# State-space scan of a bidirectional encoder block on one Trainium2 core: chunks laid out by place in their block of 8, and a scan instruction for the states between blocks

## The chip, the cores and the metric

The kernel runs on one core of one Trainium2 chip. The metric is the device time of one launch in microseconds. Three runs of the kernel before took 2667.21 to 2672.29 us, median 2671.31 us.

## The reference

One encoder layer runs on two sequences of width 1024: a prompt of 2048 positions and a sample of 512, with the same weights. Half of the mixer's channels go through a two-dimensional Fourier transform, the other half through a bidirectional state-space scan, which is what the change touches. A channel group of 16 drives 64 complex states; each state is multiplied by a constant complex number per position and gets an input added.

```python
def s5_direction(u_c, a_re, a_im, log_dt, b_re, b_im, c_re, c_im, reverse):
    lam = lax.complex(jnp.minimum(a_re, A_RE_MAX), a_im)
    dt = jnp.exp(log_dt)[:, None]
    a_bar = jnp.exp(lam * dt)
    b_bar = ((a_bar - 1.0) / lam)[..., None] * lax.complex(b_re, b_im)
    bu = jnp.einsum("blgh,gph->blgp", u_c, b_bar)
    a_seq = jnp.broadcast_to(a_bar, bu.shape)
    _, h = lax.associative_scan(_scan_combine, (a_seq, bu), axis=1, reverse=reverse)
    return jnp.einsum("blgp,ghp->blgh", h, lax.complex(c_re, c_im)).real
...
    h = rmsnorm(x, g_mix_norm) * (1.0 + scale1) + shift1
    z = h @ w_in
    y_f = fourier_mixer(z[..., :D_FOURIER], w_fourier, b_fourier)
    y_s = s5_mixer(z[..., D_FOURIER:], ...)      # y_fwd + y_bwd + D u, gelu, GLU
    merged = jnp.concatenate([rmsnorm(y_f, g_fourier_out), rmsnorm(y_s, g_ssm_out)], axis=-1)
    x = x + gate1 * (merged @ w_out)
    h = rmsnorm(x, g_mlp_norm) * (1.0 + scale2) + shift2
    ff = jnp.square(jax.nn.relu(h @ w_mlp_in + b_mlp_in)) @ w_mlp_out + b_mlp_out
    return x + gate2 * ff
```

## The kernel before

The work stands in four parts that follow one another. `mix_in` (stretch 0 to 328 us of the trace) norms the input, multiplies by `w_in`, folds the positions for the Fourier half and builds the tables of the scan: `ssm_params` (L145), `ssm_pre` (L206), and, as jobs between the folds, `scan_tables` (L123) and eight calls of `ssm_out` (L278). Then comes the scan itself together with the Fourier half (328 to 690 us), then `mix_out` (to 1117 us), then the MLP (to the end).

The scan works on columns of 8 positions. 2560 positions are 320 columns, 256 of the prompt and 64 of the sample; a matmul turns the 8 inputs of a column into its contribution to the state. The 32 channel groups go in 8 rounds `q` of `NQ = 4`. A round has a tile `V` of 128 partitions (64 states forward, 64 backward) x 2 (real, imaginary) x 4 groups x 321 columns, and these steps:

- `lead` loads the round's matrices and inputs, puts the columns in order on ScalarE (`un`), multiplies (`psV`), and copies to `V`, the backward half reversed.
- `step1` sweeps up over blocks of 8 columns, on VectorE: distances 1, 2 and 4, so that each block's last column holds the block's sum. Distance 1 is 16 instructions (L367), each multiplying by a scalar per partition and adding; distances 2 and 4 go through `axpy` (L374), which makes one complex multiply and add of four instructions (L378 to L381).
- `step2` carries the states between the 40 blocks, in two levels of 5 x 8: seven dependent `axpy` on 40 elements, then five steps on the five groups of eight (L388 to L405).
- `step3` sweeps down (distances 4, 2, 1), and three matmuls per group (`psY`) with the copies `S` of `V` give the output, which is copied (`y`) and stored.

The loop in `run` interleaves the rounds: round q's `lead`, round q-1's `step2`, round q-2's `step3`, round q's `step1`, and between them `slot`, which issues one unit of the Fourier half and of its part of the output projection (`beside`) and one column block of the conditioning matrix (`pa`). All of it is laid on the engines' queues by a scheduler (L1511) that reorders instructions when the kernel is built; every engine then runs its own queue strictly in order. The scan's pools `ssa` and `ssm` lie where the pools of `mix_in` lay (`rs.close()`, L874), so its tiles wait for the last reader of those, `ssm_out` among them. Tables go through DRAM: `ssm_out` writes `sO` on ScalarE's queue, `lead` reads it on SP's.

## Time and profile before

| | us |
|---|---|
| median of three runs | 2671.31 |
| the profiled execution's own time | 2667.14 |
| its span, first to last instruction | 2665.3 |
| TensorE (PE) busy | 2528.9 (95%) |
| VectorE (DVE) busy | 1714.6 (64%) |
| ScalarE (ACT) busy | 1277.0 (48%) |
| GpSimd (POOL) busy | 588.4 (22%) |

The profile comes from one execution. Busy time is the union of an engine's instructions; a busy TensorE may still run at the lower of its two clocks, which the granted clock tells. L numbers are lines of the kernel before; a helper's line stands for all its callers, so tiles' names tell the place.

### The profile page before, as it was taken

Reading aid. Unit: us, or ns where it says so; the run is one execution under the profiler, and the core shown is the slowest. Engines: PE = TensorE matmul, PEld = TensorE weight load, DVE = VectorE, ACT = ScalarE, POOL = GpSimd, SP = SyncE. Lnnn points to the kernel's source line nnn. Section 1 sums busy time; section 2 is a strip of 40 time slices with the busy share of each in tenths; the row PEclk is TensorE's granted clock in tenths of the full one; section 3 lists DMA queues with packets and bytes.
Section 4 is the critical chain, followed back from the end, with each engine's and each line's share of the span. In section 5 each row is a group of like instructions: output and inputs, shape, how many; then the busy total and the mean of one; then the engine's idle time right before and its main releaser. Section 6 shows DMA issues by size and latency. Waiting matters only on the chain.

```text
span 2665.3 us, 35595 instructions
## 1 busy us (share of the span) xinstructions
PE 2528.9 (95%) x12643; PEld 2285.8 (86%) x12643; DVE 1714.6 (64%) x2935; ACT 1277.0 (48%) x2227; POOL 588.4 (22%) x464
## 2 busy tenths in 40 slices
PE   6879999997999999899999999999999999999997
PEld 2767877766777878799999999999999999999997
DVE  7789599999548877446767973354346533644454
ACT  2633344544444434635544546355445573654443
POOL 3322110024355443733700001004000020130000
PEclk8979988878999999999999999999999999999999
DMA  7634476466777898777666777686667776766664
GB/s 272 209 125 144 133 233 195 151 217 237 262 264 248 296 317 291 276 245 272 226 221 221 263 256 263 222 277 231 225 223 282 242 245 227 274 229 222 229 229 163
DMA packets 276739, 623.40 MB, mean 234 GB/s; under 512 B 66256, under 2 KB 108304, under 8 KB 274768
## 3 DMA queue, kind: packets, MB, share of 16 engines
q1 hardware_dynamic: 237264, 547.16, 60.8%
q10 hardware_dynamic: 32944, 59.36, 5.9%
q0 software_dynamic: 6352, 14.60, 1.7%
q8 instruction: 100, 1.64, 0.2%
q14 instruction: 79, 0.65, 0.1%
HBM read 467.13 MB, written 153.89 MB: 233 GB/s over the span
## 4 chain that ended last, share of the span: by engine, by line
PE 49%; DVE 2%; issue 0%; ACT 0%; POOL 0%; DVEq 0%; ACTq 0%
PE acc L204 9%; PE acc L203 9%; PE acc L202 9%; PE pf L203 7%; PE pf L204 7%; PE pf L202 7%; DVE x L1439 0%; DVE big L1439 0%; PE pb L713 0%; PE pn L695 0%; DVE wl L1373 0%; DVE big L1291 0%; DVE big L1308 0%; DVE th L1324 0%; DVE ss L1277 0%
## 5 line engine op out<-in xcount | busy, mean ns | idle before, releaser
L1371 ACT CAST wh<-wr 128x512 fp32r<-128x512 f32 x672 | 414.8, 620 | 687.1 <-PE acc L203 346.7
L204 PE MATMUL pf<-th,wl 128*128 128x426 f32 (+1 forms) x1344 | 478.5, 357 | 9.1 <-POOL wl L1373 6.2
L203 PE MATMUL pf<-th,wh 128*128 128x426 f32 (+1 forms) x1344 | 481.1, 358 | 1.3 <-DVE th L1324 1.3
L202 PE MATMUL pf<-th,wh 128*128 128x426 f32 (+1 forms) x1344 | 481.0, 358 | 0.7 <-ACT x L1292 0.6
L203 PE MATMUL acc<-th,wh 128*128 128x426 f32 (+1 forms) x1344 | 478.3, 357 | 0.4 <-DVE th L1324 0.3
L202 PE MATMUL acc<-th,wh 128*128 128x426 f32 (+1 forms) x1344 | 474.5, 357 | 0.0
L204 PE MATMUL acc<-th,wl 128*128 128x426 f32 (+1 forms) x1344 | 466.9, 357 | 2.1 <-DVE wl L1373 2.0
L1391 DVE TENSOR_TENSOR big<-big,pf 128x426 f32<-128x426 f32 (+1 forms) x320 | 184.8, 596 | 250.0 <-PE pf L204 203.1
L1324 DVE TENSOR_TENSOR th<-big,th 128x1704 fp32r<-128x1704 f32 (+1 forms) x82 | 159.6, 1946 | 201.5 <-ACT th L1323 201.3
L204 PEld LDWEIGHTS pf<-th,wl 128*128 128x128 f32 x1344 | 253.8, 189 | 19.8 <-POOL wl L1373 6.9
L202 PEld LDWEIGHTS pf<-th,wh 128*128 128x128 f32 x1344 | 253.4, 189 | 11.1 <-issue 1.0
L204 PEld LDWEIGHTS acc<-th,wl 128*128 128x128 f32 x1344 | 253.2, 189 | 11.2 <-DVE wl L1373 2.8
L203 PEld LDWEIGHTS pf<-th,wh 128*128 128x128 f32 x1344 | 254.0, 189 | 10.0 <-DVE th L1324 1.5
L203 PEld LDWEIGHTS acc<-th,wh 128*128 128x128 f32 x1344 | 252.5, 188 | 9.5 <-DVE th L1324 1.1
L202 PEld LDWEIGHTS acc<-th,wh 128*128 128x128 f32 x1344 | 252.9, 188 | 9.0
L1230 POOL TENSOR_TENSOR q<-q,q 128x512 f32<-128x512 f32 x116 | 188.9, 1628 | 261.0 <-DMA q<-in_w 125.1
L709 POOL TENSOR_TENSOR r<-r,mh 128x4 f32<-128x4 f32 (+3 forms) x32 | 37.4, 1174 | 893.5 <-DVE r L708 883.9
L1398 POOL TENSOR_TENSOR big<-big 128x426 f32<-128x426 f32 (+1 forms) x128 | 144.4, 1133 | 398.2 <-ACT big L1397 397.6
L1373 DVE TENSOR_TENSOR wl<-wr,wh 128x512 fp32r<-128x512 f32 x168 | 123.3, 747 | 58.4 <-ACT wh L1371 51.5
L1323 ACT CAST th<-big 128x1704 fp32r<-128x1704 f32 (+1 forms) x82 | 132.5, 1616 | 0.7 <-PE acc L204 0.7
L1373 POOL TENSOR_TENSOR wl<-wr,wh 128x512 fp32r<-128x512 f32 x56 | 84.0, 1502 | 122.1 <-ACT wh L1371 105.9
L1324 DVE TENSOR_TENSOR th<-x,th 128x1704 fp32r<-128x1704 f32 (+1 forms) x23 | 44.6, 1938 | 83.6 <-ACT th L1323 83.6
(437 smaller groups left out, 4591.2 us busy)
## 6 DMA issues: line engine op xcount, KB each, us to landing
wl<-wL SPq DMA_DIRECT2D x224, 512.0 KB, 3.7
wr<-wS SPq DMA_DIRECT2D x192, 512.0 KB, 4.4
wr<-in_w SPq DMA_DIRECT2D x144, 512.0 KB, 4.5
wL<-wl SPq DMA_DIRECT2D x112, 512.0 KB, 2.9
q<-in_w SPq DMA_DIRECT2D x116, 256.0 KB, 4.4
wS<-q ACTq DMA_DIRECT2D x116, 256.0 KB, 3.9
wa<-in_w_ada SPq DMA_DIRECT2D x48, 512.0 KB, 5.5
big<-x1D SPq DMA_DIRECT2D x8, 1704.0 KB, 7.7
```

The source lines that it names most:

```text
L202: nc.tensor.matmul(out, l[0], r[0], start=start, stop=False)
L203: nc.tensor.matmul(out, l[0], r[1], start=False, stop=False)
L204: nc.tensor.matmul(out, l[1], r[0], start=False, stop=stop)
L709: nc.gpsimd.tensor_tensor(r[:m, js], r[:m, js], self.mh[:m, js], op=ALU.pow)
L1230: e.tensor_tensor(o, x, y, op=op)
L1323: nc.scalar.copy(th[0], src)
L1324: return th, v.tensor_tensor(th[1], src, th[0].bitcast(F32), op=ALU.subtract)
L1371: nc.scalar.copy(hi, r)
L1373: (nc.gpsimd if i % 2 and st["ph"] == 1 else v).tensor_tensor(lo, r, hi.bitcast(F32), op=ALU.subtract)
L1391: v.tensor_tensor(f[q], f[q], ps, op=op)
L1398: nc.gpsimd.tensor_tensor(f[q], f[q], f[q], op=ALU.mult)
```

## The change

Column b*8+j of a block b, place j, now lies at [j][b]: `V` is 128 x 2 x 4 x 9 x 40; a sweep at any distance takes whole runs of 40 neighbouring elements in place of every 2nd, 4th or 8th element. The order is made where `z` is stored, in the copies to `un`, and is undone in the copy to `y`; `V`, `S` keep it. The sweeps have the same number of instructions and elements as before; distance 2 is split by place and not by group.

Between blocks, `step2` turns each block's sum back by the phase that a block's constant has gained up to block b (a table of cosines and sines), runs a real first-order recurrence over the 40 blocks with one `tensor_tensor_scan` for the real and one for the imaginary part, and turns the result forward again. The multiplier of the recurrence, the constant's magnitude over 64 positions, is set to zero at blocks 0 and 32, where a sequence starts.

The table (cosine, sine, multiplier) is new: `ssm_params` computes magnitude and phase over 64 positions, `scan_tables` builds powers of the phase and, for each round, the table `RT`, which goes to DRAM (`s3`); `rload` brings a round's table back into the one tile `R` on SP's queue. The second level of powers (`BJ`) goes.

```diff
-def scan_tables(nc, tc, pk, tp, A8):
+def scan_tables(nc, tc, pk, tp, P, sR):
...
+    T4 = tp.tile([128, 4, 8, G], F32, tag="O", name="J")
+    J, K = ({k: T4[:, 2 * i + j] for j, k in enumerate("ri")} for i in range(2))
     with tc.tile_pool(name="sct", bufs=1) as tq:
-        powers(nc, tq, AJ, 0, 8)
         for k in "ri":
-            v.tensor_copy(BJ[k][:, 0], AJ[k][:, 7])
-        powers(nc, tq, BJ, 0, 8)
...
+            v.tensor_copy(J[k][:, 0], P["A8"][k][:, 0])
+        for j in (1, 2):
+            a = {x: J[x][:, j - 1] for x in "ri"}
+            cmul(nc, v, tq, J["r"][:, j], J["i"][:, j], a["r"], a["i"], a["r"], a["i"], [128, G], "pw1")
...
+        v.tensor_copy(r, J["r"][:, 0:3].rearrange("p j g -> p g j"))
+        v.tensor_scalar(i2[:, 0], J["i"][:, 0:3].rearrange("p j g -> p g j"), -1.0, None, op0=ALU.mult)
+        v.tensor_copy(i2[:, 1], J["i"][:, 0:3].rearrange("p j g -> p g j"))
+
...
+        for k in "ri":
+            v.tensor_copy(J[k][:, 1], P["U"][k])
+        powers(nc, tq, J, 1, 7)
+        cmul(nc, v, tq, K["r"][:, 1], K["i"][:, 1], J["r"][:, 7], J["i"][:, 7], J["r"][:, 1], J["i"][:, 1], [128, G], "pw1")
+        powers(nc, tq, K, 1, 4)
+    n = NQ
+    for q in range(G // n):
+        gs = slice(n * q, n * q + n)
+        T = tp.tile([128, 3, n, 40], F32, tag="o2", name="RT")
+        t = tp.tile([128, n, 40], F32, name="rt")
+        sh = [128, n, 5, 8]
+        w = lambda x: x.rearrange("p g (a j) -> p g a j", j=8)
+        ja = {k: bc(J[k][:, :, gs].rearrange("p j g -> p g j").unsqueeze(2), sh) for k in "ri"}
+        ka = {k: bc(K[k][:, 0:5, gs].rearrange("p a g -> p g a").unsqueeze(3), sh) for k in "ri"}
+        for c, (x, y, op) in enumerate((("r", "i", ALU.subtract), ("i", "r", ALU.add))):
+            v.tensor_tensor(w(T[:, c]), ja["r"], ka[x], op=ALU.mult)
+            v.tensor_tensor(w(t), ja["i"], ka[y], op=ALU.mult)
+            v.tensor_tensor(T[:, c], T[:, c], t, op=op)
+        nc.scalar.copy(T[:, 2], bc(P["R64"][:, gs].unsqueeze(2), [128, n, 40]))
+        nc.gpsimd.memset(T[:, 2, :, 0:33:32], 0.0)
+        nc.scalar.dma_start(sR[q], T)
+    return {"Ar": r, "Ai": i2}
...
+    R64, U = po.tile(sh, F32, name="R64"), {k: po.tile(sh, F32, name="U"+k) for k in "ri"}
+    v.tensor_scalar(x, x, 64.0, None, op0=ALU.mult)
+    v.tensor_scalar(th, th, 64.0, None, op0=ALU.mult)
+    exp_dve(nc, tp, R64, x, sh)
+    sincos_dve(nc, tp, U["r"], U["i"], th, sh)
...
+        un = ta.tile([128, NQ, 8, 40], F32, name="un", bufs=3)
+        nat = un[:, :, :, 0:32].rearrange("p g j (t h) -> p g t j h", h=2)
+        src = u[:, :, 0:256].rearrange("p g (t j s h) -> p g t j s h", t=4, j=8, s=4)
+        for sec, t in enumerate((slice(0, 4), slice(7, 3, -1), slice(8, 12), slice(15, 11, -1))):
+            for h in range(2):
+                nc.scalar.copy(nat[:, :, t, :, h], src[:, :, :, :, sec, h])
+        nc.scalar.copy(un[:, :, :, 32:40], u[:, :, 256:320].rearrange("p g (j c) -> p g j c", j=8))
+        un = un.rearrange("p g j b -> p g (j b)")
+
+        V = ta.tile([128, 2, NQ, 9, 40], F32, tag="V", name="V", bufs=3)
         for c in range(2):
             for j in range(NQ):
                 ps = net.ps([128, 320], "psV")
                 nc.tensor.matmul(ps, It[:, c, j], un[:, j], start=True, stop=True)
-                o = V[:, c, j, 1:321]
-                nc.scalar.copy(o[0:64], ps[0:64])
-                nc.scalar.copy(o[64:128, 0:256], ps[64:128, 255::-1])
-                nc.scalar.copy(o[64:128, 256:320], ps[64:128, 319:255:-1])
+                o = V[:, c, j, 1:9]
+                x = ps.rearrange("p (j b) -> p j b", j=8)
+                nc.scalar.copy(o[0:64], x[0:64])
+                nc.scalar.copy(o[64:128, :, 0:32], x[64:128, ::-1, 31::-1])
+                nc.scalar.copy(o[64:128, :, 32:40], x[64:128, ::-1, 39:31:-1])
+        if q == 0:
+            self.rload(0)
...
+            t4 = t.rearrange("p g (j b) -> p g j b", j=8)
+            nc.scalar.copy(t4[0:64], V[0:64, c, :, 0:8])
+            nc.scalar.copy(t4[64:128, :, :, 0:32], V[64:128, c, :, 7::-1, 31::-1])
+            nc.scalar.copy(t4[64:128, :, :, 32:40], V[64:128, c, :, 7::-1, 39:31:-1])
...
-            nc.scalar.copy(y[:, j], py)
+            nc.scalar.copy(y[:, j].rearrange("p (b j) -> p j b", j=8), py.rearrange("p (j b) -> p j b", j=8))
...
-            dst, x = V[:, :, :, o::2 * d], V[:, :, :, i::2 * d]
-            n = NQ if d == 4 else NQ // 2
-            sh = [128, 2, n, 160 // d]
-            for g in range(0, NQ, n):
-                G, r = slice(gs.start + g, gs.start + g + n), slice(g, g + n)
-                self.axpy(e, dst[:, :, r], x[:, :, r], x[:, ::-1, r], bc(P["Ar"][:, G, d - 1:d].unsqueeze(1), sh), bc(P["Ai"][:, :, G, d - 1:d], sh), sh, tag="t")
+            sh = [128, 2, NQ, 40]
+            for r in range(4 // d):
+                x = V[:, :, :, i + 2 * d * r]
+                dst = V[:, :, :, o + 2 * d * r]
+                self.axpy(e, dst, x, x[:, ::-1], bc(P["Ar"][:, gs, k:k + 1].unsqueeze(1), sh), bc(P["Ai"][:, :, gs, k:k + 1], sh), sh, tag="t")
...
-            self.sweep(b, d, b["V"][:, :, :, 1:321], True)
+            self.sweep(b, d, b["V"][:, :, :, 1:9], True)
...
-        P, tp, gs, e, n = self.P, self.tp, b["gs"], self.nc.vector, NQ
-        W = tp.tile([128, 2, n, 40], F32, tag="W", name="W")
-        W5 = W.rearrange("p c g (a b) -> p c g a b", b=8)
-        e.tensor_copy(W, b["V"][:, :, :, 8:321:8])
-        sh = [128, 2, n, 5]
-        br = bc(P["Br"][:, gs, 0:1].unsqueeze(1), sh)
-        bi = bc(P["Bi"][:, :, gs, 0:1], sh)
-        for j in range(1, 8):
-            x = W5[:, :, :, :, j - 1]
-            self.axpy(e, W5[:, :, :, :, j], x, x[:, ::-1], br, bi, sh)
...
+
+        V, R, e = b["V"], self.R, self.nc.vector
+        sh = [128, 2, NQ, 40]
+        cos, sin = (bc(R[:, i].unsqueeze(1), sh) for i in range(2))
+        T = V[:, :, :, 8]
+        W = self.tp.tile(sh, F32, name="W")
+        t1 = self.ta.tile(sh, F32, tag="ta", name="sc1")
+        t2 = self.ta.tile(sh, F32, tag="tb", name="sc2")
+        e.tensor_tensor(t1, cos, T, op=ALU.mult)
+        e.tensor_tensor(t2, sin, T[:, ::-1], op=ALU.mult)
+        for c, op in enumerate((ALU.add, ALU.subtract)):
+            e.tensor_tensor(W[:, c], t1[:, c], t2[:, c], op=op)
+        for c in range(2):
+            w = W[:, c].rearrange("p g b -> p (g b)")
+            e.tensor_tensor_scan(w, R[:, 2].rearrange("p g b -> p (g b)"), w, 0.0, op0=ALU.mult, op1=ALU.add)
+        t1 = self.ta.tile(sh, F32, tag="ta", name="sc1")
+        t2 = self.ta.tile(sh, F32, tag="tb", name="sc2")
+        e.tensor_tensor(t1, cos, W, op=ALU.mult)
+        e.tensor_tensor(t2, sin, W[:, ::-1], op=ALU.mult)
+        for c, op in enumerate((ALU.subtract, ALU.add)):
+            e.tensor_tensor(V[:, c, :, 0, 1:40], t1[:, c, :, 0:39], t2[:, c, :, 0:39], op=op)
+        e.memset(V[:, :, :, 0, 0:33:32], 0.0)
+        if b["q"] + 1 < 32 // NQ:
+            self.rload(b["q"] + 1)
+
+    def rload(self, q):
+        self.R = self.ta.tile([128, 3, NQ, 40], F32, name="R")
+        self.nc.sync.dma_start(self.R, self.sR[q])
...
-                    nc.scalar.copy(z, ps.rearrange("p (n t) -> p t n", t=8))
+                    nc.scalar.copy(z.rearrange("p t (j c) -> p t j c", j=8), ps.rearrange("p (c j t) -> p t j c", j=8, t=8))
...
-            jobs = [lambda: P.update(scan_tables(nc, tc, spp, po, P["A8"]))]
+            jobs = [lambda: P.update(scan_tables(nc, tc, spp, po, P, self.sD[3]))]
```

Where instructions stand now. The first place is VectorE's queue at the end of the table build. Before, the build of the powers (`BJ`, L49 to L142, `cm` are scratch tiles) ran straight into the first `ssm_out` (L288):

```order
L53 TENSOR_TENSOR cm3_1753<-J_1690 128x128 [waits DVE_49]
L54 TENSOR_TENSOR cm4_1754<-J_1690 128x128
L140 COPY BJr_1764<-J_1690 128x256
L55 TENSOR_TENSOR J_1690<-cm3_1753,cm4_1754 128x128 [waits DVE_49]
L141 TENSOR_SCALAR BJi_1765<-J_1690 128x256 [waits DVE_49]
L142 COPY BJi_1765<-J_1690 128x256
L288 TENSOR_TENSOR O_1769<-Cr_241,PWor_418 128x512 [waits DVE_49]
L288 TENSOR_TENSOR O_1769<-nCi_242,PWor_418 128x512
```

Of the change, one round's table `RT` is followed by the next (L159 to L161 write the two rows of a table; `rt` is scratch, `J` the powers):

```order
L161 TENSOR_TENSOR RT_1880<-RT_1880,rt_1881 128x160 [waits DVE_49]
L160 TENSOR_TENSOR rt_1881<-J_1760 128x160 [waits DVE_49]
L161 TENSOR_TENSOR RT_1880<-RT_1880,rt_1881 128x160 [waits DVE_49]
L160 TENSOR_TENSOR rt_1892<-J_1760 128x160 [waits DVE_49]
L159 TENSOR_TENSOR RT_1891<-J_1760 128x160 [waits DMAHW5_49,Activation_49]
L159 TENSOR_TENSOR RT_1891<-J_1760 128x160
L161 TENSOR_TENSOR RT_1891<-RT_1891,rt_1892 128x160 [waits DVE_49]
L160 TENSOR_TENSOR rt_1892<-J_1760 128x160 [waits DVE_49]
```

The eight rounds' tables stand one behind the other, each waiting for the DMA that stored the one before; the 48 instructions of `ssm_out` come behind all of them, where before they stood among the folds.

The second place is VectorE's queue at the first instruction of the scan. Before, it follows the last step of `mix_in` (L199 and L898 split `fh` and `Ze`):

```order
L878 MEMSET e96_2962 128x768 [waits DVE_49]
L882 COPY e96_2962<-ee_1287 128x8x2 [waits DVE_49]
L882 COPY e96_2962<-ee_1287 128x8x2 x2
L199 TENSOR_TENSOR fh_2968<-e96_2962,fh_2967 128x768 [waits PE_49,Activation_49]
L898 TENSOR_TENSOR Ze352_107<-pe_2935,Ze352_107 32x258 [waits Activation_49]
L367 SCALAR_TENSOR_TENSOR V_3412<-V_3412,AJr_1759 128x160 [waits DMAHW2_49,DMAHW3_49,DMAHW1_49,DMAHW4_49,DMAHW0_49,Activation_49]
L367 SCALAR_TENSOR_TENSOR V_3412<-V_3412,AJr_1759 128x160 [waits Activation_49]
```

In the change (L403 is the first sweep, L317 and L318 the last `ssm_out`, L227 splits of the Fourier half's `cw` and `Z`):

```order
L317 TENSOR_TENSOR o2_3094<-Cr_242,PWoi_420 128x512 [waits DVE_49]
L318 TENSOR_TENSOR O_3089<-O_3089,o2_3094 128x512 [waits DVE_49]
L227 TENSOR_TENSOR cw11_3204<-pc_3413,cw10_3203 128x512 [waits Activation_49]
L939 TENSOR_TENSOR cw3_3209<-pc_3422,cw3_3209 32x512 [waits Activation_49]
L227 TENSOR_TENSOR cw21_3206<-pc_3431,cw20_3205 128x512 [waits Activation_49]
L227 TENSOR_TENSOR cw31_3208<-pc_3440,cw30_3207 128x512 [waits Activation_49]
L227 TENSOR_TENSOR Z1_3211<-zin_3451,Z0_3210 128x2x256 [waits DMAHW0_49,Activation_49]
L227 TENSOR_TENSOR Z1_3211<-zin_3455,Z0_3210 128x2x256 [waits DMAHW3_49,Activation_49]
L403 SCALAR_TENSOR_TENSOR V_3593<-V_3593,AJr_1786 128x4x40 [waits DVE_49,Activation_49]
L403 SCALAR_TENSOR_TENSOR V_3593<-V_3593,AJr_1786 128x4x40 [waits Activation_49] x3
```

The first sweep has moved behind the first units of the Fourier half (`cw`, `Z1`) and behind `ssm_out`.

The third place is SP's queue after the first round's `step2`, in the change alone (`wa` is the conditioning matrix, `fD` the Fourier half's output, L448 `rload`):

```order
L1086 DMA fD_68<-yF_3564 128x128 [waits DMAHW1_49,DVE_49,Activation_49]
L1086 DMA fD_68<-yF_3563 128x128 [waits DMAHW2_49,DVE_49]
L448 DMA R_3878<-s3_72 128x480 [waits DMAHW3_49,DVE_49]
L679 DMA wa_3924<-in_w_ada 128x1024 [waits DMAHW4_49,PE_49]
L1086 DMA fD_68<-yF_3667 128x512 [waits DMAHW5_49,DVE_49]
```

The load of the next round's table waits for VectorE's last read of `R`, and the loads of `wa` and the stores of `fD` stand behind it.

## Rows read from the trace of the kernel before

**Rows 1.** Stretches of the span: each engine's busy time and instructions.
```profile
core 0: us, PE busy (x) PEld busy (x) DVE busy (x) ACT busy (x) POOL busy (x), PEclk, DMA share, GB/s
0.00:140.00 140.00, 111.27 (x525) 74.35 (x526) 107.29 (x288) 69.73 (x178) 52.32 (x66) 0.90 0.72 236
140.00:283.00 143.00, 118.95 (x640) 103.64 (x640) 130.61 (x176) 46.23 (x81) 37.41 (x21) 0.86 0.39 123
283.00:328.00 45.00, 40.24 (x274) 36.56 (x273) 19.71 (x23) 16.91 (x36) 6.19 (x2) 1.00 0.50 165
328.00:690.00 362.00, 330.19 (x1543) 265.00 (x1542) 343.94 (x1019) 173.21 (x422) 66.46 (x53) 0.81 0.63 209
690.00:1117.00 427.00, 398.98 (x1795) 331.68 (x1794) 281.96 (x361) 194.34 (x312) 198.94 (x123) 0.96 0.83 281
1117.00:2665.00 1548.00, 1529.30 (x7874) 1474.62 (x7873) 831.05 (x1073) 776.56 (x1201) 227.10 (x201) 1.00 0.69 239
```
**Rows 2.** VectorE's groups from 328 to 690 us: the sweeps.
```profile
line engine op names shapes xcount | busy us, mean ns | idle before us <-releasers
L367 DVE SCALAR_TENSOR_TENSOR V<-V,AJr 128x160 f32<-128x160 f32 x128 | 54.2, 459 | 6.3 <-ACT V L322 6.0
L367 DVE SCALAR_TENSOR_TENSOR V<-V,AJi 128x160 f32<-128x160 f32 x128 | 44.8, 395 | 0.0
L381 DVE TENSOR_TENSOR V<-V,sc 128x320 f32<-128x320 f32 x48 | 38.0, 792 | 0.2
L379 DVE TENSOR_TENSOR sc<-AJi,V 128x320 f32<-128x320 f32 x48 | 36.4, 759 | 0.0
L378 DVE TENSOR_TENSOR sc<-AJr,V 128x320 f32<-128x320 f32 x48 | 36.3, 755 | 0.2
L380 DVE TENSOR_TENSOR sc<-sc,sc 128x320 f32<-128x320 f32 x48 | 24.5, 510 | 0.1
```
**Rows 3.** The same view: first and last of the sixteen groups of `step2`.
```profile
L378 DVE TENSOR_TENSOR sc<-BJr,W 128x40 f32<-128x40 f32 x56 | 16.2, 289 | 0.4
...
L396 DVE MEMSET V<- 128x16 f32 x8 | 0.6, 72 | 0.0
```
**Rows 4.** VectorE in order of time from 500.31 us; first columns start and duration.
```profile
start us, us, engine line op out<-in xcount [idle before <-releaser]
500.31 0.48 DVE L380 TENSOR_TENSOR sc<-sc,sc 128x320 f32<-128x320 f32 x1
500.71 0.28 DVE L199 TENSOR_TENSOR X<-px,X 128x128 fp32r<-128x128 f32 x1
500.91 0.18 DVE L380 TENSOR_TENSOR sc<-sc,sc 128x40 f32<-128x40 f32 x1
501.02 0.72 DVE L381 TENSOR_TENSOR V<-V,sc 128x320 f32<-128x320 f32 x1
501.66 0.71 DVE L379 TENSOR_TENSOR sc<-AJi,V 128x320 f32<-128x320 f32 x1
502.29 0.23 DVE L381 TENSOR_TENSOR W<-W,sc 128x40 f32<-128x40 f32 x1
502.44 0.73 DVE L378 TENSOR_TENSOR sc<-AJr,V 128x320 f32<-128x320 f32 x1
503.08 0.68 DVE L367 SCALAR_TENSOR_TENSOR V<-V,AJr 128x160 f32<-128x160 f32 x2
503.68 0.22 DVE L378 TENSOR_TENSOR sc<-BJr,W 128x40 f32<-128x40 f32 x1
```
**Rows 5.** PE's waits from 328 to 690 us: the longest.
```profile
PE psY L346 <- ACT S L341: 14.9, 3, 13.5
```
**Rows 6.** VectorE's queue from 23.4 us.
```profile
23.39 0.18 DVE L177 TENSOR_TENSOR pmkr<-pmkr,pminv 128x32 f32<-128x32 f32 x1
23.49 0.19 DVE L55 TENSOR_TENSOR Pi<-cm,cm 128x32 f32<-128x32 f32 x1
27.02 0.69 DVE L751 TENSOR_TENSOR ss<-ss,sqk 128x512 f32<-128x512 f32 x1 [3.34 <-ACT sqk L749]
```
**Rows 7.** The line that stores `ssm_out`'s table: issue and landing.
```profile
L291 ACTq DMA_DIRECT2D s<-O x8: 326/326/327, 149.0 to 262.0; - x8
...
DMA to landing us min/median/max: 2.6/2.9/9.1
```
**Rows 8.** VectorE's waits from 283 to 328 us: the longest.
```profile
DVE fh L199 <- ACT fh L198: 22.6, 4, 15.3
```
**Rows 9.** The DMA queue's waits from 328 to 690 us, one on VectorE.
```profile
SPq L1045 <- DVE yF L1036: 25.9, 7, 5.2
```

More of the change, by code (lines that the diff above doesn't have):

```diff
@@ L143, in scan_tables @@
-    return out
+            v.tensor_copy(J[k][:, 0], P["A8"][k][:, 0])
+        for j in (1, 2):
+            a = {x: J[x][:, j - 1] for x in "ri"}
+            cmul(nc, v, tq, J["r"][:, j], J["i"][:, j], a["r"], a["i"], a["r"], a["i"], [128, G], "pw1")
+        r = pk.tile([128, G, 3], F32, name="AJr")
+        i2 = pk.tile([128, 2, G, 3], F32, name="AJi")
+        v.tensor_copy(r, J["r"][:, 0:3].rearrange("p j g -> p g j"))
+        v.tensor_scalar(i2[:, 0], J["i"][:, 0:3].rearrange("p j g -> p g j"), -1.0, None, op0=ALU.mult)
@@ new lines, in scan_tables @@
+        v.tensor_copy(i2[:, 1], J["i"][:, 0:3].rearrange("p j g -> p g j"))
+        for M in (J, K):
+            v.memset(M["r"][:, 0], 1.0)
+            v.memset(M["i"][:, 0], 0.0)
+        for k in "ri":
[19 more added lines that the diff above has]
+        nc.scalar.dma_start(sR[q], T)
@@ L332, in step3 @@
         for d in (4, 2, 1):
-            self.sweep(b, d, V[:, :, :, 0:320], False)
+            self.sweep(b, d, V[:, :, :, 0:8], False)
         S = []
```

42 lines of the change are left out of this document (5 added, 37 removed).

## The prediction

> **What bounds the kernel now.** I read the stretches of the span first [rows 1]. [...] From 328 to 690 us, where the scan runs, it is 330.2 x 0.81 = 267 of 362 us, 74%, while VectorE is busy for 343.9 us, 95%. [...] So VectorE sets this stretch, and 362 - 267 = 95 us is the most that relief can return. From 140 to 283 us VectorE is nearly as full (130.6 of 143 us, 91%, TensorE 102), and the 45 us after that are TensorE's (40.2 at full clock, VectorE free for 25 us, 22.6 of them in waits for ScalarE's splits [rows 8]). From 690 to 1117 us VectorE is busy 66% and TensorE does 383 of 427 us, 90%: this shows what the program reaches when VectorE is not full.
>
> Second I read VectorE's groups in the scan's stretch [rows 2, 3], and third its order of time [rows 4], since durations overlap and only the distance from one start to the next is what an instruction takes from the queue. Tiles of 320 neighbouring elements (L380) take 0.40 us; the other three of an `axpy`, which touch every 4th or 8th element of `V`, take 0.64, 0.63 and 0.64 us. The two L367 take 0.60 us, 0.30 each, on 160 elements two apart. A neighbouring 128 takes 0.20 us (L199), so by the slope to 320 a neighbouring 160 takes about 0.235 us.
>
> **Sweeps.** Their count stays: 192 `axpy` instructions and 256 of L367 [rows 2]. Before: 144 x 0.64 + 48 x 0.40 + 256 x 0.30 = 92 + 19 + 77 = 188 us. After, if runs of 40 go as neighbours: 192 x 0.40 + 256 x 0.235 = 77 + 60 = 137 us. The other end is no gain: nothing in the trace shows this shape of runs, and it could be the three dimensions of the pattern that cost the 0.24 us. I take 137, because L381 on `W`, with elements eight apart, also pays (0.15 us against 0.11 for L380 on a neighbouring 40 [rows 4]), which goes with distance.
>
> [...]
>
> **step2.** It goes as 424 instructions in 16 groups that add up to 103 us [rows 3], of which the first and the last stand there. They overlap by about 0.08 us each (0.23 against 0.15 for L381 [rows 4]), 34 us, so some 69 us. In its place come per round four products of 320 elements (0.40), four sums of about 160 (0.235), a memset (0.07) and two scans. No row shows a scan. Its bounds are 0.235 us, as one neighbouring 160, and 0.64 us, as the slowest 320; I take 0.40, near the middle. That is 1.6 + 0.94 + 0.07 + 0.8 = 3.4 us, 27 us in eight rounds (24 to 31).
>
> [...]
>
> **VectorE's sum.** The rest of its 344 us, 344 - 188 - 69 = 87 us, stays. After: 137 + 27 + 87 = 251 us, 93 less.
>
> **The stretch.** TensorE's 267 us stay. With TensorE at 90%, as after 690 us, it would take 297 us; but VectorE would then be 85% busy, and not 66. On a line between the two stretches (95% busy goes with 74, 66% with 90) the time that fits itself is 320 us: VectorE 78%, TensorE 83%. I take 310, a gain of 52 us (42 to 65). What is late next is then TensorE itself, and in each round the path from the last sweep over ScalarE's copies `S` to `psY`, which before cost TensorE one idle of 13.5 us [rows 5].
>
> Beside these 251 us lies more work that I cost at nothing. ScalarE gets four more copies per round, half as large, and two more dimensions in others; it is busy 173 of 362 us [rows 1], and 10 us more leave it at 59% of 310. The load of `R` (seven of eight wait for VectorE on SP's queue, in front of `wa`, `fD` and `zin`) is one more wait of a kind the queue has: seven waits of `fD` for L1036 took 25.9 us, at most 5.2 each [rows 9]. `wa` is loaded two blocks ahead, which covers that; if the cover is gone, up to 5 us in some rounds, 10 us in all. `R` itself is needed only a round later.
>
> **Table build.** In `ssm_params` 49 instructions of 128x32 are new, 0.10 us each from start to start [rows 6], 5 us; the same place has 3.3 us idle. I count +2 (0 to 5). In `scan_tables` come 48 products and sums of 160 elements, 0.235 us or, with the penalty of distance (0.12), 0.355 us: 11 to 17 us, and some twelve small ones more, 1.5 us. The tables go through one tile, so each waits until the one before is stored. By the store of `ssm_out` that is 0.33 us of issue and 2.9 us to landing [rows 7], and with ScalarE's copy, the memset and the semaphores about 4 us; the slowest landing, 9.1 us, makes it 10. In VectorE's queue some four or five of these waits have next to nothing in front of them, so 16 to 20 us of waiting. Behind the waiting table stand `h1` of the projection and the folds' splits, for which TensorE waits.
>
> Two things stand against this. The last tables stand beside the last folds, where VectorE had 25 us free. And the 48 instructions of `ssm_out` (128x512, about 0.61 us as L751 with its overlap [rows 6], 29 us) leave the full stretch of 140 to 283 us and come later, when TensorE has the first units of the Fourier half to do. I count 0 for both together, from -14 (half of `ssm_out`'s 29 us is returned) to +20 (all waits count).
>
> **Sum.** 2667.1 - 52 + 2 + 0 = 2617 us for an execution like the profiled one, whose time is 2667.14 us with 1.8 us around the span. The median of three stands 4.2 us above it, so 2621.
>
> **The rivals.** (A) *TensorE becomes the only bound*, and the lighter queue before 283 us is returned in full: 65 + 12 us of gain, 2594. For it: the clock, which is 0.96 to 1.00 wherever TensorE is kept fed [rows 1]. Against it: VectorE would still be 85% busy, and eight chains over three engines remain.
>
> (B) *The sweeps don't get faster*, since the shape and not the distance costs. Then VectorE has 302 us, the line gives 343 us for the stretch, and the time is 2667 - 19 + 2 + 4 = 2654. For it: a run of 40 is short, and two dimensions stand above it. Against it: rows 4, as above.
>
> (C) *No change*: the chain of a round (matmul, ScalarE's copies, up, between, down, copies, matmul) sets the pace, and VectorE was full only because the scheduler filled its gaps. For it: the 13.5 us of rows 5. Against it: VectorE waited at the sweeps for ScalarE only 6.3 us in all [rows 2].
>
> (D) *Slower*: the table build holds VectorE's queue. If landings go as the slowest (10 us per wait, five bare waits) and the folds stand behind them, it costs 50 + 13 us before the first fold's end. It decides from 8 us a wait on: 5 x 8 + 13 + 2 = 55 against 52. At 10 us and with the stretch at 320 us the time is 2667 + 63 + 2 - 42 + 4 = 2694. For it: order, and one slow landing in eight. Against it: the median of 2.9 us.
>
> **Chances.** My forecast 0.50, A 0.20, B 0.14, C 0.05, D 0.11. The forecast's own range is 2600 to 2645. Left out of the range may be the fastest part of A (below 2580) and C and D above 2662, some 0.2. About 0.2%, 5 us, is what this kernel's measurement can tell from no change: faster 0.84, the same 0.05, slower 0.11.
>
> **What would show it.** In the changed profile the `axpy` groups of 320 elements should all stand near 0.48 us (0.40 apart) and L403 near 0.32 us, the scans under 0.5 us; from the first sweep to the last VectorE should be about 80% busy with TensorE's clock near 0.9; and before the first sweep VectorE should show waits on the stores of `RT` of about 4 us, four or five of them. Wrong would be: strided times kept (B); VectorE idle in the scan while the stretch stays at 350 us or more (C); waits on `RT` of 8 us or more with TensorE idle behind them (D).

## The result and the profile after

The changed kernel takes 2685.7 us, median of four runs (2681.7 to 2687.3), against 2669.4 us for the kernel before: ratio 1.0058, interval 1.0041 to 1.0076. It is 16 us slower; 2621 us were forecast, and the range ended at 2662.

The profiled execution took 2685.62 us, 18.5 us more than that of before. By stretch of the span, in the columns of [rows 1]:

```profile
326.00:390.00 64.00, 39.26 (x200) 33.42 (x200) 30.54 (x58) 16.57 (x49) 8.32 (x14) 0.71 0.82 265
390.00:715.00 325.00, 301.68 (x1400) 240.67 (x1400) 274.25 (x662) 187.85 (x433) 60.85 (x45) 0.83 0.66 227
715.00:1060.00 345.00, 320.54 (x1444) 259.60 (x1442) 234.35 (x313) 151.61 (x234) 145.29 (x92) 0.98 0.82 271
```

From the first `psV` (390.2 us, 327.7 before) to the last `psY` the scan now takes 325 us; before it took 367. But it starts 62 us later, and in the 64 us ahead of it TensorE has only 39.26 x 0.71 = 28 us of work (busy time times granted clock, an estimate). VectorE is down to 84% in the scan, while TensorE does 301.68 x 0.83 = 250 of 325 us, 77%: hardly more than the 74% of before [rows 1].

Why it starts late stands in VectorE's order of time (start, duration):

```profile
288.22 0.33 DVE L161 TENSOR_TENSOR RT<-RT,rt 128x160 f32<-128x160 f32 x1
288.47 0.69 DVE L316 TENSOR_TENSOR O<-Cr,PWor 128x512 f32<-128x512 f32 x1
...
366.81 0.69 DVE L318 TENSOR_TENSOR O<-O,o 128x512 f32<-128x512 f32 x1
...
392.19 0.39 DVE L403 SCALAR_TENSOR_TENSOR V<-V,AJr 128x160 f32<-128x160 f32 x1 [1.91 <-ACT V L355]
```

The powers J and K lie in the one buffer of tag "O", which `ssm_out`'s tile O uses too, and are read until the last of the eight RT rounds. So the first `ssm_out` starts when the last RT is done, at 288 us; before, all eight ran between 145.6 and 262 us. Then they follow one another through the one O until 367 us, and only when the last is stored is the memory free in which the scan's tiles lie. The last store lands at 373.8 us, and the scan's first loads are issued on SP's queue at 376 us. In that queue five loads of the Fourier half stand in front, the last of which waits for TensorE's `pc` until 374.3 us; memory and queue come free within 1 us of each other, so this trace alone does not tell which of them set the start. Two runs below do: e5 moves `ssm_out` alone and the start goes with it, e13 takes the table out and the start is back.

```profile
338.69 36.18 SPq L998 DMA_DIRECT2D zin<-in_f_ch  x5
376.05 0.42 SPq L333 DMA_DIRECT2D It<-s  x1
377.00 0.88 SPq L335 DMA_DIRECT2D u<-uD  x1
```

VectorE's groups from 390 to 715 us, which answer to [rows 2, 3]:

```profile
L403 DVE SCALAR_TENSOR_TENSOR V<-V,AJr 128x160 f32<-128x160 f32 x128 | 53.4, 456 | 21.7 <-ACT V L355 21.1
L403 DVE SCALAR_TENSOR_TENSOR V<-V,AJi 128x160 f32<-128x160 f32 x128 | 43.7, 383 | 0.0
L416 DVE TENSOR_TENSOR sc<-sc,sc 128x320 f32<-128x320 f32 x48 | 29.4, 612 | 0.8
L415 DVE TENSOR_TENSOR sc<-AJi,V 128x320 f32<-128x320 f32 x48 | 27.5, 574 | 0.0
L414 DVE TENSOR_TENSOR sc<-AJr,V 128x320 f32<-128x320 f32 x48 | 27.3, 569 | 0.3
L417 DVE TENSOR_TENSOR V<-V,sc 128x320 f32<-128x320 f32 x48 | 27.2, 567 | 0.8
...
L435 DVE TENSOR_TENSOR_SCAN W<-R,W 128x160 f32<-128x160 f32 x16 | 7.0, 474 | 0.0
...
L432 DVE TENSOR_TENSOR W<-sc,sc 128x160 f32<-128x160 f32 x16 | 4.5, 320 | 0.2
```

By mean duration three of the four `axpy` groups fell from 0.76 to 0.57 us, the fourth (`sc<-sc,sc`) rose from 0.51 to 0.61, `step2` fell from 103 us to some 34 us of durations, the d = 1 sweeps (L403) not at all. The means hide two kinds of instruction. Most stand as here (start, duration):

```profile
445.52 0.48 DVE L415 TENSOR_TENSOR sc<-AJi,V 128x320 f32<-128x320 f32 x1
445.92 2.46 DVE L403 SCALAR_TENSOR_TENSOR V<-V,AJr 128x160 f32<-128x160 f32 x8
448.29 0.49 DVE L414 TENSOR_TENSOR sc<-AJr,V 128x320 f32<-128x320 f32 x1
```

That is 0.48 us of duration and 0.40 us to the next start for an `axpy` instruction, and 2.37 us for eight of L403, 0.30 each. The others ran beside GpSimd:

```profile
667.18 0.48 DVE L415 TENSOR_TENSOR sc<-AJi,V 128x320 f32<-128x320 f32 x1
667.25 1.55 POOL L1271 TENSOR_TENSOR q<-q,q 128x512 f32<-128x512 f32 x1 [5.21 <-issue]
667.69 1.45 DVE L416 TENSOR_TENSOR sc<-sc,sc 128x320 f32<-128x320 f32 x1
668.96 2.82 POOL L1271 TENSOR_TENSOR q<-q,q 128x512 f32<-128x512 f32 x2 [0.17 <-POOL q L1271]
669.18 1.46 DVE L417 TENSOR_TENSOR V<-V,sc 128x320 f32<-128x320 f32 x1
```

Of the 192 `axpy` instructions of the sweeps 18 took 1.43 to 1.59 us, each of them beside GpSimd's products `q`; of the 156 that had no GpSimd instruction beside them none took over 0.50 us.

For comparisons I use marks that hold for every kernel: the last `pe` (last product of `mix_in`), the first `pgate` (first product after the scan and the Fourier half's `pof`), and the first `pf` (start of the MLP). The count of TensorE's instructions between two marks differs by under 1% between kernels, so the time between them compares directly. Before and after:

```profile
333.00:790.00 457.00, 416.19 (x1906) 333.10 (x1905) 386.68 (x1074) 216.58 (x490) 114.34 (x80) 0.84 0.66 221
790.00:1044.00 254.00, 244.06 (x1088) 199.03 (x1087) 197.22 (x258) 110.46 (x167) 114.36 (x72) 0.97 0.85 285
```

```profile
332.00:798.00 466.00, 413.46 (x1912) 331.44 (x1910) 338.44 (x763) 243.88 (x543) 97.12 (x77) 0.84 0.70 237
798.00:1061.00 263.00, 243.09 (x1089) 197.60 (x1090) 196.43 (x260) 110.49 (x167) 117.34 (x74) 0.97 0.84 281
```

So of the 18.5 us, 9 come between `pe` and `pgate`, 8 to 9 in the stage behind it, which the change doesn't touch, and 2 in the MLP; 1 us is won before `pe`. VectorE is busy 48 us less between `pe` and `pgate`, although the late `ssm_out` now stands partly there, and ScalarE 27 us more.

### The profile page after: what moved, and what is told of

It is laid out like the page before. It is cut to its first block, busy times and chain, and to the rows that moved or that the text cites. A ratio compares the mean times of both kernels' runs of the same rounds, so it can differ in the third digit from the quotient of the medians.

```text
span 2683.8 us, 35478 instructions
## 1 busy us (share of the span) xinstructions
PE 2528.9 (94%) x12643; PEld 2287.7 (85%) x12643; DVE 1666.4 (62%) x2709; ACT 1301.1 (48%) x2267; POOL 571.6 (21%) x472
## 4 chain that ended last, share of the span: by engine, by line
PE 48%; DVE 2%; DMA 0%; issue 0%; ACT 0%; POOL 0%; DVEq 0%; ACTq 0%
PE acc L232 9%; PE acc L231 9%; PE acc L230 9%; PE pf L231 7%; PE pf L232 7%; PE pf L230 7%; DVE x L1480 1%; DVE big L1480 0%; PE pb L754 0%; DVE wl L1414 0%; DMA wr<-wS 0%; DVE th L1365 0%; PE pn L736 0%; DVE big L1349 0%; DVE big L1332 0%; DVE big L1391 0%
## 5 line engine op out<-in xcount | busy, mean ns | idle before, releaser
L1271 POOL TENSOR_TENSOR q<-q,q 128x512 f32<-128x512 f32 x116 | 178.1, 1535 | 267.7 <-DMA q<-in_w 141.8
```

Of the source, the lines that this page charges most:

```text
L1271: e.tensor_tensor(o, x, y, op=op)
```

## The experiments

All kernels by these marks, in us. "Start" is the first `psV` counted from the last `pe`; "DVE" is VectorE's busy time from `pe` to `pgate`; the ratio is to the kernel before on the same chip. A profile is of one execution: those of e3, e8, e9 and e14 took 16, 9, 8 and 6 us more than the median of their runs, so their marks may be high by as much.

| kernel | ratio, 95% | last pe | start | pe to pgate | DVE | pgate to pf |
|---|---|---|---|---|---|---|
| before | 1 | 333 | -5 | 457 | 387 | 254 |
| after | 1.0058 (1.0041-1.0076) | 332 | +58 | 466 | 338 | 263 |
| e5_before_late_out | 1.0173 (1.0153-1.0193) | 321 | +42 | 509 | 408 | 260 |
| e1_own_tiles | 1.0147 (1.0132-1.0163) | 371 | -5 | 448 | 325 | 266 |
| e6_hold | 1.0159 (1.0142-1.0176) | 371 | -4 | 447 | 319 | 267 |
| e7_hold_pool | 1.0161 (1.0144-1.0177) | 377 | -4 | 447 | 322 | 265 |
| e13_no_table | 1.0047 (1.0031-1.0062) | 342 | -4 | 451 | 319 | 269 |
| e9_swap | 1.0036 (1.0022-1.0050) | 332 | +74 | 472 | 340 | 261 |
| e12_swap3_pool | 1.0135 (1.0113-1.0157) | 327 | +96 | 502 | 329 | 261 |
| e15_own_compact | 1.0042 (1.0027-1.0057) | 338 | +32 | 466 | 326 | 260 |
| e16_un_on_pool | 1.0034 (1.0020-1.0048) | 341 | +33 | 458 | 341 | 261 |
| e3_scan_alone | 1.0251 (1.0220-1.0283) | 370 | -4 | 485 | 364 | 269 |
| e8_old_layout_hold_pool | 1.0207 (1.0180-1.0234) | 376 | -4 | 473 | 362 | 263 |
| e14_old_layout_no_table | 1.0064 (1.0045-1.0084) | 334 | -4 | 474 | 365 | 264 |
| e4_no_step2 | 1.0135 (1.0119-1.0150) | 373 | -5 | 443 | 299 | 264 |
| e17_before_no_step2 | 1.0017 (1.0003-1.0031) | 334 | -5 | 456 | 335 | 264 |
| e18_before_no_sweeps | 0.9884 (0.9870-0.9899) | 332 | -4 | 419 | 200 | 269 |

**Four at first.** My theory (M) was the late start; rivals were the table's own work (T), SP's queue (Q) and the scan itself (S, L, V, P); each text set off below says, before its run, what a theory's letter means and expects.

e1_own_tiles, J and RT in tiles of their own:

```diff
-    T4 = tp.tile([128, 4, 8, G], F32, tag="O", name="J")
+    T4 = tp.tile([128, 4, 8, G], F32, name="J")
-        T = tp.tile([128, 3, n, 40], F32, tag="o2", name="RT")
+        T = tp.tile([128, 3, n, 40], F32, name="RT", bufs=2)
```

> The changed kernel, but the table of powers J has a tile of its own (not the one that ssm_out's O uses) and RT has two tiles of its own (not the one of ssm_out's o2). Theory M (shared tiles hold ssm_out behind all eight table rounds, so the memory of the scan comes free 62 us later): the first psV returns from 390 us to about 330 us, and the time falls by the 62 us less the 28 us of other TensorE work that stood in the hole and has to run later: 2685 - 34 = about 2650, between 2635 and 2660. Theory T (the table's own VectorE work and store round trips in front of the folds cost it, wherever the tiles lie): first psV stays beyond 370 us and the time at 2675 to 2690. Theory Q (SyncE's queue is blocked by the loads of the f_ch maps, not by memory): first psV stays beyond 370 us, 2675 to 2690.

The late start is gone and the kernel is slower still, 2710 us: nobody's expectation. The last `pe` comes 39 us later. `ssm_out`, free of J, was put at 42 to 152 us, ahead of `ssm_pre`; and the 7.9 kB more pushed `wfold`'s tiles onto memory that `ssm_pre` holds: the cast in front of their first split, on ScalarE at 170.8 us, was released by `ssm_pre`'s `Mh`. The split stands at 175.86 us; before, it stood at 75.23.

```profile
175.86 0.68 DVE L227 TENSOR_TENSOR we<-wf,we 128x514 fp32r<-128x514 f32 x1
```

e3_scan_alone: the same with the layout taken back (V as 321 columns, strided sweeps), `step2` reading `V[:, :, :, 8:321:8]`.

> The old layout of the chunks (blocks of 8 neighbours, sweeps on elements 16 and 32 bytes apart) with the new step2 (turn, two scan instructions, turn back) and with J and RT in tiles of their own. It is the first experiment without the new layout, so the difference of the two is what the layout is worth. Theory L (the layout gives the d = 4 and d = 2 sweeps 0.64 to 0.49 us and the d = 1 sweeps nothing, and dearer copies on ScalarE take part of that back): this kernel 5 to 25 us slower than the first experiment. Theory 0 (the layout is worth nothing, since the chain of a round and ScalarE set the pace): within 4 us of it. If the layout costs more on ScalarE than it gives on VectorE: faster than the first experiment by over 4 us.

2734 us, 24 us over its pair, as L has it (37 us between the marks, in an execution 16 us above the median).

e4_no_step2: the first experiment with `step2` reduced to

```diff
+        e.memset(V[:, :, :, 0], 0.0)
```

> The first experiment with the work of step2 left out (the states that pass between blocks are set to zero, so nothing is turned, scanned or turned back; the output is not the reference's). It takes 27 us of VectorE work and the link between the up and the down sweeps out of the scan stretch. Theory V (VectorE still sets the pace of the scan stretch): 20 to 27 us faster than the first experiment. Theory P (with VectorE at 84% busy, TensorE's side work and ScalarE's copies set the pace): within 8 us of the first experiment, and VectorE's busy share in the stretch falls to about 77%.

2706 us, 4 us under its pair: P. VectorE is busy 26 us less (299 of 443 us), and the stretch is 5 us shorter.

e5_before_late_out, the late order of `ssm_out` alone in the kernel before:

```diff
+                if t == order[4]:
+                    v.tensor_copy(po.tile([128, 8], F32, tag="O", name="hold"), p[:, :, 0])
-                for job in jobs[2 * it:2 * it + 2]:
+                for job in (jobs[:1] if it == 0 else jobs[1:] if it == 4 else []):
```

> The kernel before, scan and layout untouched, with one thing added: ssm_out's tile O is first taken by a small tile that is written at about 282 us in the folds of the last chunk, so all eight ssm_out run after that as in the changed kernel. Theory M (the late start alone is what costs): the first psV moves from 328 to 375 to 395 us and the time is 20 to 40 us over the kernel before (2690 to 2710). Theory T or S (the cost lies in the table's work or in the scan itself): within 8 us of the kernel before.

2716 us, 46 over before, more than M's 20 to 40. The first `psV` comes at 364 us:

```profile
321.00:830.00 509.00, 423.22 (x1914) 339.25 (x1912) 407.91 (x1091) 224.47 (x511) 110.37 (x81) 0.82 0.65 215
```

`ssm_out` now runs until 346 us, with no table in the kernel, and the stretch takes 52 us more. Its late VectorE work lies in that stretch too (VectorE is busy 21 us more), so the start's own share is not apart. That the late order is expensive is shown; what it costs in the changed kernel is not yet.

**The late start taken from the changed kernel.** e6_hold and e7_hold_pool keep the tiles of e1 and hold `ssm_out` back until AJi is done; e7 also builds RT on GpSimd (`v.tensor_tensor` of the rounds becomes `nc.gpsimd.tensor_tensor`):

```diff
+        v.tensor_copy(tp.tile([128, 3], F32, tag="O", name="hold"), i2[:, 1, 0])
```

> In the first experiment ssm_out, freed of J, went to 42 to 152 us, ahead of ssm_pre, and TensorE's first two stages came 39 us later. Here J and RT keep tiles of their own, and a tile of 3 columns (hold), written when the table AJi is done, takes ssm_out's tile O until then, so that ssm_out falls between the folds, as in the kernel before. All RT rounds stay on VectorE. Theory M (what costs is that ssm_out and with it the memory of the scan come late; VectorE has room for the table between the folds): the last pe at 332 to 340 us, first psV at 330 to 345, time 2650 to 2665. Theory T (27 us of RT work and 33 us of ssm_out cannot both stand in VectorE's queue in front of the folds): the last pe at 350 to 365 us and the time at 2675 to 2695.

> The same with the 48 products and sums of RT on GpSimd instead of VectorE. GpSimd is busy for 31 us of the 133 us from 200 to 333 us in the changed kernel, and took 1.2 to 1.6 us for 128x512. Both theories expect the table to be out of the way of the folds here: the last pe at 332 to 345 us, first psV at 330 to 350 us. By the TensorE time lost in the scan stretch (94 us before, 86 in the first experiment) the time is then 8 to 12 us under the kernel before: 2655 to 2665. If the time is over 2675 although psV starts by 345 us, theory M falls, and the new scan is itself slower than the old.

2715 and 2716 us. The last `pe` stays at 371 and 377 us, with 21 us of RT on VectorE between 150 and 260 us or with none: not T as it was put, but again `wfold` behind `ssm_pre` (e7 is no clean test of T: beside a busy GpSimd VectorE's own instructions took longer, as said at the end). e7's clause "over 2675 although psV starts by 345" did not apply, since it started at 374.

e8_old_layout_hold_pool is e7 with the layout of e3.

> The same again with the old layout (sweeps on elements 16 and 32 bytes apart), so only step2 and its table differ from the kernel before. The difference to the run with the layout is the worth of the layout, without the late start. From the pair of the first experiments (2734 and 2710): 24 us slower than with the layout, so 2680 to 2690. If step2 alone is what gives (76 us less VectorE work in it): 2650 to 2665, no slower than with the layout.

2728 us, 12 over its pair where 24 were expected; neither 2680 to 2690 nor the other time came.

e13_no_table needs no more memory: it stores a constant in place of the table.

```diff
+    T = tp.tile([128, 3, NQ, 40], F32, tag="o2", name="RT")
+    nc.gpsimd.memset(T, 0.5)
+    for q in range(G // NQ):
+        nc.scalar.dma_start(sR[q], T)
```

> In the runs with tiles of their own, the wider tables pushed the tiles of wfold (we) onto memory that ssm_pre frees only at the end, and the folds came 40 us later: those runs mix two causes. This one takes no more memory than the changed kernel: the building of the table is left out (J's and K's powers and the eight RT rounds; one tile of 0.5 is stored eight times in their place, so the output is not the reference's), and the scan, the layout and step2 stay as they are. Theory M (the new scan is good for 8 to 16 us, and the shared tiles take it back): the last pe at 330 to 336 us, ssm_out at 145 to 265 us, first psV at 325 to 340, TensorE time lost from the last pe to the last psY 78 to 87 us (94 before), time 2652 to 2664. Theory S (the new scan is itself no faster): lost 92 to 100 us, time 2668 to 2680.

```profile
342.00:793.00 451.00, 417.41 (x1906) 335.44 (x1904) 318.94 (x738) 235.08 (x519) 104.25 (x81) 0.84 0.71 230
793.00:1062.00 269.00, 246.35 (x1088) 198.91 (x1088) 200.78 (x259) 109.93 (x168) 105.06 (x70) 0.96 0.83 268
```

The scan starts ahead of the last `pe` and gives 6 us between the marks, but 9 us are lost before the first (`ssm_out` runs until 307 us, the cause was not followed), 14 behind the second and 4 in the MLP: 2688 us. What TensorE loses up to the last `psY`, 348 - 325 x 0.81 = 85 us, is M's; neither M's total nor S's came. With no table and no late start the change is still no faster.

e14_old_layout_no_table is e13 with the layout of e3.

> The same without the table, with the old layout; so only step2 differs from the kernel before in the scan (its table, left out, costs nothing here). The two runs with the old layout so far lost 119 and 111 us of TensorE time in the scan, and lay 24 and 12 us over their pairs. By those: 12 to 24 us over the run with the layout, 2668 to 2685, so step2 alone gives nothing and the layout is what gives. If step2's 76 us of VectorE work are what gives: 2650 to 2662, no slower than with the layout.

2691 us, 3 over its pair in all where 12 to 24 were expected, but 23 us more between the marks (474).

e9_swap splits off the table and runs it after `ssm_out` (`jobs += [lambda: turn_tables(nc, tc, po, P, self.sD[3])]` behind the eight); e12_swap3_pool does so with `jobs[3 * it:3 * it + 3]` and RT on GpSimd.

> The whole of the change with no more memory, in another order: the tiles O and o2 go to AJr and AJi first, then to ssm_out, and last to J, K and the eight RT rounds (as jobs of the last chunk's folds). Theory M: ssm_out at 145 to 265 us as in the kernel before, RT from about 290 to 345 us on an emptier VectorE, the memory of the scan free at about 350 instead of 374 us, first psV at 355 to 365 (390 in the changed kernel) and the time 10 to 20 us under the changed kernel: 2665 to 2675. Theory T (the table's own work costs it, wherever it stands): 2682 to 2692.

> The same order, with three jobs to a chunk instead of two and RT's products and sums on GpSimd, each round some 4 to 5 us of it. Theory M: VectorE is free of the table, but the rounds take GpSimd 35 to 40 us from about 300 us and the memory comes free no sooner: first psV at 350 to 370, time 2662 to 2678. Theory T: 2682 to 2692.

2682 and 2713 us. Neither starts as early as expected: J's powers began at about 300 us and RT took until 386 and 408, so the scan starts 74 and 96 us after `pe`. The stretch grows with that, 472 and 502 us. e9's 2682 lies at the edge of T's range, but the start was late here too, so it does not speak for T.

e15_own_compact: J and K in 3.3 kB of their own, RT after `ssm_out`, by turns in two tiles.

```diff
+    T4 = tp.tile([128, 26, G], F32, name="J")
+        T = tp.tile([128, 3, n, 40], F32, tag=("o2", "O")[q % 2], name="RT")
```

> The whole change with its table so built that nothing has to wait for it: J and K in a tile of 3.3 kB of their own (little enough that wfold's tiles stay where they are), ssm_out in O and o2 behind the small tile hold, and then the RT rounds, by turns in o2 and O. Theory M2 (the late start costs 18 us, and the new scan is good for 5 to 10 us of TensorE time between the last pe and the first pgate): last pe at 328 to 336 us, first psV at 338 to 355, from the last pe to the first pgate 446 to 455 us (457 before, 466 in the changed kernel), time 2666 to 2678, which is the kernel before within 0.3%. Theory V (VectorE set the pace of the scan, and its 95 us less are worth 40 to 60 us once the start is early): 2620 to 2645.

2687 us: not V, but not M2 either. The RT rounds hold the tiles O and o2 until 353 us, the start is still 32 us late, and the stretch takes 466 us as in the changed kernel.

e16_un_on_pool puts one line of e15, the copies of `un`, on `nc.gpsimd.tensor_copy`.

> The same with the 64 small copies of un (0.45 us each on ScalarE, 29 us) on GpSimd. Theory A (ScalarE sets the pace of the scan now: its copies of V, S, y and un stand in one queue): 10 to 25 us under the run before this one. Theory C (no engine alone sets it; TensorE runs at half its clock for about 110 to 140 us of it, after waits on either): within 6 us; if GpSimd's copies are 2 us each, slower by 5 to 15 us, since psV waits for un.

2685 us, the same within the intervals, though 8 us shorter between the marks. The time goes with C; a part of ScalarE in the stretch is possible.

**VectorE taken out of the kernel before.** e17_before_no_step2 replaces `step2` by a memset of the blocks' starts, e18_before_no_sweeps also drops the sweeps of d = 4 and 2:

```diff
+        e.memset(b["V"][:, :, :, 0:320:8], 0.0)
```

```diff
         if d > 1:
+            return
```

> The kernel before with step2 left out (the states between blocks are set to zero; the output is not the reference's). It takes 103 us of VectorE work out of the scan stretch, more than the change, and moves nothing else. By the prediction's own step (VectorE 95% busy sets the stretch of 362 us; with 95 us less TensorE gets along at 86%): 45 to 60 us faster, 2610 to 2625. Theory C (VectorE was busy but not the bound; TensorE's queue stood 91% busy, much of it at half its clock): 0 to 15 us faster.

> The kernel before with step2 and the sweeps of d = 4 and d = 2 left out (only the d = 1 sweeps remain; the output is not the reference's): some 240 of the 347 us of VectorE work of the scan stretch. By the prediction's step: down to the time that TensorE alone needs, 80 to 95 us faster. Theory C: VectorE's queue is nearly empty here, so what is left is TensorE with its clock and ScalarE's copies: 15 to 35 us faster. If it is under 10 us, VectorE had no part in the stretch at all.

```profile
334.00:790.00 456.00, 420.07 (x1903) 336.84 (x1901) 335.18 (x658) 216.61 (x490) 113.60 (x81) 0.85 0.68 223
```

```profile
332.00:751.00 419.00, 394.98 (x1908) 321.40 (x1906) 199.54 (x466) 217.57 (x490) 106.33 (x81) 0.89 0.73 243
```

This settles the first step. With all of `step2` gone VectorE is busy 52 us less, in the changed kernel 48, and the stretch takes 456 us for 457: nothing. The kernel as a whole takes 5 us more, 2678, since the stage behind grew by some 9. With 187 us less the stretch gives 38 us, and the kernel 30.

In the prediction's own stretch, from the first `psV` to the last `psY`, the kernel before, e17 and e18 show:

```profile
327.70:695.10 367.40, 335.59 (x1563) 268.95 (x1563) 348.61 (x1023) 177.04 (x428) 70.75 (x55) 0.81 0.63 209
328.30:686.20 357.90, 331.10 (x1524) 266.18 (x1524) 284.37 (x602) 173.33 (x424) 67.73 (x51) 0.81 0.63 207
328.50:640.70 312.20, 304.77 (x1523) 250.72 (x1523) 157.90 (x415) 175.57 (x426) 50.69 (x47) 0.86 0.70 233
```

In e17 VectorE falls from 95% to 79% busy, where the prediction's line has TensorE at 83%; TensorE goes from 74% to 75%. At 51% (e18) TensorE reaches 84%. The scan's own span does shrink, by 9 us and in e18 by 55, but from the last `psY` to `pgate` it then takes 10 and 16 us more (94 before): TensorE's other work, which stood beside the scan, has to be done behind it (408 and 410 matmuls there, 369 before).

**Second profiles**, of the two kernels unchanged:

> The kernel before once more, unchanged, for a second profile. The stage from the first pgate to the first pf took 254.5 us in the kernel before and 260 to 269 us in every other kernel run here, also in those whose edit ends long before it. If that is the program (another order of the same instructions in that stage), it takes 253 to 257 us again; if it is how one execution fell out, 258 to 268. The stretch from the last pe to the first pgate, which the argument rests on: 455 to 459 us.

> The changed kernel once more, unchanged, for a second profile: the stretch from the last pe to the first pgate 464 to 468 us, and from there to the first pf 261 to 265 us, if both are the program's own.

```profile
332.00:790.00 458.00, 417.18 (x1904) 332.61 (x1902) 386.86 (x1074) 216.72 (x490) 116.67 (x79) 0.84 0.66 220
790.00:1042.00 252.00, 243.39 (x1088) 198.85 (x1088) 192.15 (x257) 109.53 (x166) 116.08 (x73) 0.97 0.86 287
```

```profile
331.00:794.00 463.00, 408.24 (x1912) 329.04 (x1910) 339.03 (x763) 243.37 (x543) 98.50 (x77) 0.85 0.72 238
794.00:1057.00 263.00, 244.01 (x1088) 198.87 (x1088) 196.31 (x259) 110.30 (x168) 116.27 (x74) 0.96 0.85 282
```

Both marks repeat within 3 us (252 and 463 lie 1 us outside what was expected), so the 8 to 10 us from `pgate` to `pf` are the program's own. That stage has the same 1088 matmuls in both programs, in another order from the twentieth group of equal ones on: the scheduler plans the whole program anew for each edit. In the changed kernel and all 15 edited ones it took 260 to 269 us, 264 in e17, though nothing of the scan's table is in that one. So a stage that an edit does not touch moves by 5 to 16 us with the plan (that the order alone does it was not tested), and differences of that size between the marks can be the plan's too.

## Why the prediction was wrong

**The step that failed** is the first: "VectorE sets this stretch, and 362 - 267 = 95 us is the most that relief can return", with the line from 95% busy and 74% to 66% and 90%. A high busy share was taken for the bound. e17 shows it false on the kernel before: 52 us less of VectorE between the marks (48 in the changed kernel, 62 to 68 in e1, e6, e7 and e13, where `ssm_out` is out of the way), and no gain, where the line gave 45 to 60 us. TensorE's queue was no less full (416 of 457 us), and what it lost there went to idle time (41 us) and more to the granted clock, 0.84: 416 x 0.84 = 350, so 66 us by this estimate. The prediction's 267 us are the same product, 330.2 x 0.81 [rows 1], an estimate too; no run shows the scan's stretch at a granted clock of 1.00 (e18 reached 0.86 there). VectorE's relief changed neither loss: idle time is 36 us in e17 and the clock 0.85. Only with 187 us less (e18) did both losses fall, to 24 us idle and a clock of 0.89, for 38 us of the stretch.

**Rival C** had half of the mechanism (VectorE full without setting the pace), at 0.05; that the chain of a round sets it is not shown. I argued against it with VectorE's small waits (6.3 us at the sweeps). That it showed few waits because its neighbours ran late too is my guess, and was not tested.

**The sign** came by a way that no rival had. D expected waits on the stores of RT in VectorE's queue; they sum to 3.3 us for L159, not 16 to 20. The second step that failed is "0 for both together": that `ssm_out` comes later was counted as a gain of up to 14 us, and that the scan's start hangs on it was left out. What it cost is the order of tiles: `ssm_out` behind the last RT, and behind it the memory of the scan. In e1, e6, e7 and e13, which start the scan early, the stretch took 447 to 451 us. Against the two profiles of either kernel (457 and 458, 466 and 463), the late start costs the changed kernel 12 to 19 us, and the new scan by itself gives 6 to 11. These four differ in more than the start, in e15 and e9 the stretch did not follow the start evenly (466 at 32, 472 at 74 us), and a new plan alone moves as much, so both are estimates. The remaining 8 to 10 us are the stage `pgate` to `pf`.

**The terms.** `axpy` was right: forecast 0.48 us of duration and 0.40 from start to start, measured 0.48 to 0.49 (medians of the four groups) and 0.40, or 0.51 to 0.53 where the next instruction reads the result, as for the products with R; the means of 0.57 to 0.61 come from the 18 that ran beside GpSimd. L403: forecast 0.32, measured 0.456 and 0.383 as means, as before; it stands 0.30 us from start to start in both layouts, so neither distance nor shape set it, and 17 us of the 93 are missing. The forecast took its 0.235 us from products and sums, which do reach it (L432, 0.24), and not from this kind of instruction. The old `step2` was counted at 69 us; without it (e17) VectorE is busy 52 us less. The new one: forecast 27 us, measured 34 us of durations, and 26 us less without it (e4 against e1). The scan stands 0.40 us from start to start, where a sum of as many elements (L432) stands 0.24; 0.40 is just the value picked between its bounds without a row, which is luck. Of the signs named, VectorE came near (84% busy in the scan, 80 forecast), and TensorE's clock did not (0.83, near 0.9 forecast): the work went away and the time did not follow.

**Distance.** Three of the four `axpy` instructions, whose elements lay 16 or 32 bytes apart, went from 0.64 to 0.40 us from start to start as neighbours, as forecast. L403, whose elements lay 8 bytes apart (L367), stands 0.30 us as before and gained nothing; the prediction put the step from 0.235 to 0.30 us down to distance, which was the error. In the table, the products that read powers 128 bytes apart (L159) stand 0.36 us from start to start (median of 16), near the 0.355 of the forecast's upper end.

**What I left out.** ScalarE: I counted four more copies per round, 10 us. The `y` copies, now permuted, went from 429 to 786 ns (L347, L383), and `un` from 32 copies of 402 ns to 64 of about 450; ScalarE is busy 27 us more between the marks. What that costs is open: e16 took `un` from it, the stretch was 8 us shorter and the kernel's time the same.

**Open.** Why the stretch with the new `step2` in the old layout (473, 474) takes 17 us more than with the old one (457), or with none at all (456), was not found; 6 to 9 us of that may be the executions that were profiled, and some the plan. Nor was what holds TensorE's granted clock at 0.83 in the scan, and whether its many short waits do; in the kernel before the longest is the 13.5 us of [rows 5].

None of the versions that compute the whole beats the kernel before.

## What to carry to other kernels

Before counting on relief of an engine that is 95% busy, leave its work out and run that: here it would have shown in one run that 52 us less buy nothing. Take the time to a mark behind all work that must be done: the scan's own span shrank in each of these runs, and part of what it gave up, in e17 all of it, came back behind it. And before putting a new table into a tile that is "free", follow who has that tile next and what memory waits behind it; a tile of its own can cost as much when it moves other tiles in memory.
